# Indexer scores of a hybrid decoder step: from stacked 128-row products to pairs of 64-row tiles

## The chip, the core and the metric

One Trainium2 chip, of which one core runs the program. The metric is the device time of one execution in microseconds (us). TensorE is called PE in the profile (its weight loads are PEld), VectorE DVE, ScalarE ACT, GpSimd POOL, and SyncE SP.

## The reference, cut to what matters

One decoder layer runs over a prompt of 2048 positions and over 8 samples of 8 new positions each. The change is in the indexer, which scores every earlier key for each query and keeps the best 256:

```python
def indexer_scores(qi, wi, ki):          # 8 indexer heads x 64, one shared 64-wide key
    dots = jnp.einsum('bthd,bld->bthl', qi, ki)
    return jnp.einsum('bth,bthl->btl', wi, jax.nn.relu(dots))
```

For a block of 128 queries and L keys this is eight products with a contraction of 64, a relu each, and a weighted sum over the heads. Around it stand a combined input projection (2048 x 1024 by 1024 x 3656), attention over the chosen keys, a spatial gating group, an output projection and a gated embedding.

## The kernel before

All products are made to float32 accuracy out of float32r operands. A number is held as a rounded high part and the rest, its low part (`split`, lines 122 to 124: ACT makes the high part, DVE the low one), and the products of the parts are summed in PSUM.

The program has three phases. Phase A projects the 17 blocks (16 of the prompt, b = 0 to 15, and the samples) in three rounds (`ROUNDS`), chunk of columns by chunk of columns (`CH`, 14 of them). For each block and chunk, `proj` (lines 303, 304 and 306) runs 24 products of 128 rows into the PSUM tile `z`. In between, `pump` (in `phase_a`) feeds in steps of two chains: `idx`, which makes the scores of a block, and `topk`, which finds the 256th best score and writes a mask. Phase B does attention, phase C the output. The order in which the instructions finally stand on each engine is set by a list scheduler, which works with modelled times and moves an instruction to where it takes its operands and buffers to be ready. The five engines then run their lists in that order and wait for each other by semaphores.

In `idx` before, the key tile `ki_stack` holds the high parts of the 64 key components in rows 0 to 63 and the low parts in rows 64 to 127. The query of a head is loaded twice side by side, transposed and split (tiles `qih` and `qil`, lines 646, 123, 124). One product of 128 rows with `qih` (line 661) gives high x high plus high x low, a second with `qil` (line 662) gives low x high plus low x low. A head's scores for up to 1024 keys fill one buffer of the PSUM tile `dots`, of which there are two. ACT applies relu in place (line 664), and DVE adds the head to the score tile `big` (line 666) and so frees the buffer. The scores begin as minus the key's number times a tiny unit, made by POOL (line 652) from an int16 tile `iota` that is filled once (line 480).

Blocks 2 to 15 go through `idx`: 14 blocks with 3 to 16 times 128 keys, 133 x 128 = 17,024 keys in all. With 8 heads and 2 products this is 272,384 columns, in 608 products.

Of the kernel before, what the change touches and what calls it, by code (L numbers as in the profile page):

```python
# [9 lines left out]
F32 = mybir.dt.float32  # L10
F32R = mybir.dt.float32r
# [3 lines left out]
AF = mybir.ActivationFunctionType  # L15
OP = mybir.AluOpType
# [5 lines left out]
SEQ = 2048  # L22
NB = 16
SB = 16
PAST = 1024
WS = PAST + 64
# [4 lines left out]
UNIT = float(2.0 ** -110)  # L31
# [79 lines left out]
class Builder:  # L111
# [80 lines left out]
    def phase_a(self, eb):  # L192
        tc, nc, I, O = self.tc, self.nc, self.I, self.O
        with ExitStack() as es:
# [7 lines left out]
            ac = right("a_const", 1)  # L202
# [3 lines left out]
            hp = pool("a_h", 6)  # L206
# [23 lines left out]
            ident = self.ident  # L230
# [79 lines left out]
            later = []  # L310
# [19 lines left out]
            def post(name, b, z):  # L330
                P = self.rows(b)
                rt = ropet[:, b]
                if name == "x1":
                    w = z[:, 64:72]
                    if b == SB:
                        nc.vector.tensor_scalar(self.absw[:P, b], w, (8 * 64) ** -0.5, None, op0=OP.mult)
                    else:
                        nc.scalar.activation(self.absw[:P, b], w, AF.Abs, scale=(8 * 64) ** -0.5)
                        nc.scalar.activation(self.sgn[:P, b], w, AF.Sign)
                    kin2 = wk.tile([128, 2, 64], F32, name="kin")[:P]  # L340
                    nc.scalar.activation(kin2, z[:, None, 0:64].to_broadcast([P, 2, 64]), AF.Copy)
                    self.rope(nc.vector, kin2, rt, 2, wk, P)
                    kin = kin2[:, 0]
                    dst = O["idx_k_sample"].rearrange("o a t d -> (o a t) d") if b == SB else O["idx_k_prompt"][0, 0, b * 128:(b + 1) * 128]
                    nc.sync.dma_start(dst, kin)

                    def ki_t():
                        ps = self.tp.tile([128, 4, 128], F32, name="tp")
                        nc.tensor.transpose(ps[:, 0, :P], kin2.rearrange("p a d -> p (a d)"), ident[:P, :P])
# [4 lines left out]
                    later.append(ki_t)  # L354
# [74 lines left out]
            blocks_due, dots, tops = [], [], []  # L429
# [36 lines left out]
            for b in ROUNDS[0][1:]:  # L466
# [12 lines left out]
            iota = ac.tile([128, SEQ], mybir.dt.int16, name="iota")  # L479
            nc.gpsimd.iota(iota, pattern=[[1, SEQ]], base=0, channel_multiplier=0)  # L480
            self.iota = iota
# [81 lines left out]
            order = list(range(NB)) + [SB]  # L563
# [61 lines left out]
    def load_qi(self, b):  # L625
# [7 lines left out]
            out.append(qd)  # L633
        return out

    def idx(self, b):
        nc, wk, wk2 = self.nc, self.wk, self.wk2
        W = 128 * (b + 1)
        qds = self.load_qi(b)
        yield None  # L640
        qh, ql = [], []
        for j in range(2):
            qd = qds[j].rearrange("p h a d -> p h (a d)")
            ps = self.tp.tile([128, 4, 128], F32, name="tp")
# [5 lines left out]
            yield 2  # L650
        acc = self.big.tile([128, SEQ], F32, name="big")[:, :W]
        nc.gpsimd.tensor_scalar(acc, self.iota[:, :W], -UNIT, 1.0, op0=OP.mult, op1=OP.mult)
        kf = self.ki.rearrange("p a b -> p (a b)")
        for c0 in range(0, W, 1024):
            cn = min(1024, W - c0)
            for h in range(8):
                ps = self.dp.tile([128, 1024], F32, name="dots")
                for s0 in range(0, cn, 512):
                    sn = min(512, cn - s0)
                    rhs = kf[:, c0 + s0:c0 + s0 + sn]  # L660
                    nc.tensor.matmul(ps[:, s0:s0 + sn], lhsT=qh[h // 4][:, h % 4], rhs=rhs, start=True, stop=False)  # L661
                    nc.tensor.matmul(ps[:, s0:s0 + sn], lhsT=ql[h // 4][:, h % 4], rhs=rhs, start=False, stop=True)  # L662
                r = ps[:, :cn]
                nc.scalar.activation(r, r, AF.Relu)  # L664
                a = acc[:, c0:c0 + cn]
                nc.vector.scalar_tensor_tensor(a, r, self.sgn[:, b, h:h + 1], a, op0=OP.mult, op1=OP.add)  # L666
# [11 lines left out]
    def sample_idx(self):  # L678
        nc, wk2, I = self.nc, self.wk2, self.I
        V = nc.vector  # L680
        qi = wk2.tile([128, 4, 128], F32R, name="qih", bufs=3).bitcast(F32)
# [16 lines left out]
        pick = wk2.tile([128, 4, 128], F32R, name="qih", bufs=3)  # L698
# [7 lines left out]
        ps = self.tp.tile([128, 4, 128], F32, name="tp")  # L706
# [3 lines left out]
        ps = self.tp.tile([128, 4, 128], F32, name="tp")  # L710
# [5 lines left out]
        V.tensor_copy(knT, ps[:, 0, :64])  # L716
        yield 2
        acc = self.big.tile([128, SEQ], F32, name="big")
        pgs = {}

        def fetch(i):
# [8 lines left out]
        scs, behind = {}, []  # L730

        def second(c, p, n, kT):
            ds = self.tp.tile([128, 4, 128], F32, name="tp").rearrange("p a b -> p (a b)")[:, :n]
            nc.tensor.matmul(ds, lhsT=qi[:, p], rhs=kT[:, :n], start=True, stop=True)
            r = wk2.tile([128, 4, 128], F32R, name="qil", bufs=3).bitcast(F32).rearrange("p a b -> p (a b)")[:, :n]
            nc.scalar.activation(r, ds, AF.Relu)
            behind.append(lambda: third(c, p, n, r))

        def third(c, p, n, r):
            if p == 0:  # L740
                scs[c] = self.dp.tile([128, 1024], F32, name="dots")
            nc.tensor.matmul(scs[c][:64, :n], lhsT=G[:, p], rhs=r, start=(p == 0), stop=(p == 3))
            if p == 3:
                V.scalar_tensor_tensor(acc[:64, c * 512:c * 512 + n], self.iota[:64, c * 512:c * 512 + n], -UNIT,
                                       scs.pop(c)[:64, :n], op0=OP.mult, op1=OP.add)

        for c in range(3):
            n = 512 if c < 2 else 64
            for p in range(4):
                old = list(behind)  # L750
                behind.clear()
                for f in old:
                    f()
                if c < 2:
                    fetch(c * 4 + p + 1)
                    pg = pgs.pop(c * 4 + p)
                    ps = self.tp.tile([128, 4, 128], F32, name="tp")
                    for k in range(4):
                        nc.tensor.transpose(ps[:, k], pg[:, k].rearrange("p a d -> p (a d)"), self.ident)
                    kT = wk2.tile([128, 4, 128], F32R, name="qih", bufs=3).bitcast(F32).rearrange("p a b -> p (a b)")  # L760
# [788 lines left out]
```

## Time and profile before

| | us |
|---|---|
| Three timed runs | 1964.53, 1956.28, 1952.77 |
| Median of the three | 1956.28 |
| Span of the profiled execution, first to last instruction | 1952.4 |
| PE busy in it | 1865.8 (96%) |
| DVE, ACT, POOL busy | 1317.3, 995.7, 830.4 |
| Mean granted clock of TensorE, as a share of full speed | 0.985 |

No time of its own is given for the profiled execution beside its span; the median of the timed runs is 3.9 us above that span. Busy times of PE come from modelled ends: two products that follow each other overlap in the records, so what a product costs is read from the distance between two starts.

### The profile page before, as it was taken

How to read it: one execution, taken by the hardware profiler on the slowest of the kernel's cores; microseconds unless marked ns; L12 is line 12 of the kernel's file. 1: busy time of each engine (PE TensorE's matmuls, PEld its weight loads, DVE VectorE, ACT ScalarE, POOL GpSimd, SP SyncE). 2: the span in 40 equal slices, each digit the busy share in tenths (PEclk: the TensorE clock that was granted, in tenths of full speed). 3: DMA queues.
4: the chain of work that ended last, by engine and by line, in shares of the span. 5: the costliest groups of instructions: out<-in, count | busy, mean ns of one | idle time of the engine just before them, and what ended most of it. 6: DMA issues, size and time to landing. Idle time of an engine off the chain costs nothing. (4 is left out here: it accounts for less than half of the span.)

```text
span 1952.4 us, 35414 instructions
## 1 busy us (share of the span) xinstructions
PE 1865.8 (96%) x12370; PEld 1655.2 (85%) x12370; DVE 1317.3 (67%) x3682; ACT 995.7 (51%) x1907; POOL 830.4 (43%) x1323
## 2 busy tenths in 40 slices
PE   6989999899999899998999899999999999999998
PEld 5989989897998898997999778887788877888887
DVE  5496566488889758889752688888878865333321
ACT  3234325245555535665664788777867753122211
POOL 5482565554335679547513452213211155222311
PEclk9999999899999999998999999999999999999999
DMA  6423324423333432433455442222222064222311
GB/s 197 112 68 91 113 86 140 125 57 101 85 102 103 144 100 76 126 96 100 135 187 173 142 125 81 81 72 85 64 70 60 27 212 148 90 99 74 116 37 44
DMA packets 193687, 202.26 MB, mean 104 GB/s; under 512 B 85528, under 2 KB 160864, under 8 KB 193376
## 3 DMA queue, kind: packets, MB, share of 16 engines
q1 hardware_dynamic: 187872, 181.08, 30.9%
q0 software_dynamic: 5632, 18.88, 3.1%
q8 instruction: 98, 1.61, 0.4%
q14 instruction: 85, 0.70, 0.1%
HBM read 142.47 MB, written 57.42 MB: 102 GB/s over the span
## 5 line engine op out<-in xcount | busy, mean ns | idle before, releaser
L303 PE MATMUL z<-whi,hhi 128*128 128x256 f32 (+1 forms) x1792 | 461.3, 291 | 14.2 <-ACT qn L376 4.2
L304 PE MATMUL z<-wlo,hhi 128*128 128x256 f32 (+1 forms) x1792 | 455.0, 287 | 2.4 <-POOL wlo L276 2.4
L303 PEld LDWEIGHTS z<-whi,hhi 128*128 128x128 f32 x1792 | 342.7, 191 | 26.7 <-ACT qn L376 6.7
L304 PEld LDWEIGHTS z<-wlo,hhi 128*128 128x128 f32 x1792 | 342.7, 191 | 6.5 <-POOL wlo L276 2.7
L306 PE MATMUL z<-whi,hlo 128*128 128x256 f32 (+1 forms) x1792 | 269.6, 287 | 0.0
L275 POOL TENSOR_SCALAR whi<-raw 128x256 fp32r<-128x256 f32 (+1 forms) x332 | 151.2, 466 | 265.0 <-PE z L306 115.7
L306 PEld LDWEIGHTS z<-whi,hlo 128*128 128x128 f32 x1792 | 240.1, 189 | 4.8
L666 DVE SCALAR_TENSOR_TENSOR big<-dots,sgn,big 128x1024 f32<-128x1024 f32 (+7 forms) x176 | 178.7, 1016 | 43.3 <-ACT dots L664 42.6
L664 ACT ACTIVATE dots<-dots 128x1024 f32<-128x1024 f32 (+7 forms) x176 | 140.5, 801 | 118.4 <-PE dots L662 115.2
L124 DVE TENSOR_TENSOR b_pt<-b_tp,b_pt 128x512 fp32r<-128x512 f32 (+1 forms) x288 | 183.4, 656 | 14.1 <-ACT b_pt L123 12.0
L802 ACT ACTIVATE bfw<-big,tk 128x384 bf16<-128x384 f32 (+14 forms) x105 | 136.6, 1301 | 93.5 <-DVE tk L822 58.7
L123 ACT ACTIVATE b_pt<-b_tp 128x512 fp32r<-128x512 f32 (+1 forms) x288 | 156.1, 579 | 54.2 <-PE b_tp L1111 51.3
L1128 PE MATMUL b_o<-b_pt,Vst 128*128 128x512 f32 x544 | 182.9, 422 | 0.6 <-DVE b_pt L124 0.5
L1085 ACT ACTIVATE b_sm<-b_sm,b_st 128x128 f32<-128x128 f32 (+15 forms) x128 | 155.2, 1214 | 34.7 <-DVE b_st L1078 33.5
L1111 PE MATMUL b_tp<-mats,b_sm 128*128 128x128 f32 x1088 | 171.7, 274 | 0.3 <-ACT b_sm L1085 0.2
L1111 PEld LDWEIGHTS b_tp<-mats,b_sm 128*128 128x128 f32 x1088 | 132.2, 141 | 30.0 <-ACT b_sm L1085 2.0
L276 POOL TENSOR_TENSOR wlo<-raw,whi 128x256 fp32r<-128x256 f32 (+1 forms) x182 | 144.5, 803 | 6.2
L1076 PE MATMUL b_s<-Kst,b_qh 128*128 128x512 f32 (+3 forms) x320 | 139.8, 439 | 6.7 <-DVE b_st L1078 4.8
L1078 DVE CUSTOM_DVE_ANT_0 b_sm<-b_s,b_mask,b_st 128x512 f32<-128x512 f32 (+3 forms) x192 | 124.0, 646 | 23.9 <-PE b_s L1077 19.9
L661 PE MATMUL dots<-ki_stack,qih 128*128 128x512 f32 (+3 forms) x304 | 113.6, 376 | 10.7 <-DVE big L666 10.7
L1077 PE MATMUL b_s<-Kst,b_ql 128*128 128x512 f32 (+3 forms) x320 | 117.9, 371 | 0.1
L662 PE MATMUL dots<-ki_stack,qil 128*128 128x512 f32 (+3 forms) x304 | 111.9, 378 | 0.0
(344 smaller groups left out, 4095.4 us busy)
## 6 DMA issues: line engine op xcount, KB each, us to landing
raw<-w_in SPq DMA_DIRECT2D x336, 128.0 KB
x<-x_prompt SPq DMA_DIRECT2D x16, 512.0 KB
b_qr<-s_q SPq DMA_DIRECT2D x32, 256.0 KB
s_r<-hlo SPq DMA_DIRECT2D x32, 256.0 KB
c_r<-s_r SPq DMA_DIRECT2D x16, 512.0 KB
c_x<-x_prompt SPq DMA_DIRECT2D x16, 512.0 KB
y_prompt<-c_rn SPq DMA_DIRECT2D x15, 512.0 KB
qid<-s_qi SPq DMA_DIRECT2D x56, 128.0 KB
```

Source lines behind the costliest of these rows:

```text
L123: nc.scalar.activation(hi, src, AF.Copy)
L124: nc.vector.tensor_tensor(lo, src, hi.bitcast(F32), OP.subtract)
L275: nc.gpsimd.tensor_scalar(wh[:, k, :n], raw[:, :n], 1.0, 1.0, op0=OP.mult, op1=OP.mult)
L276: (nc.vector if k < WLO_DVE[r] else nc.gpsimd).tensor_tensor(wl[:, k, :n], raw[:, :n], wh[:, k, :n].bitcast(F32), OP.subtract)
L303: nc.tensor.matmul(z, lhsT=hh[:, k], rhs=wh[:, k, :n], start=(k == 0), stop=False)
L304: nc.tensor.matmul(z, lhsT=hh[:, k], rhs=wl[:, k, :n], start=False, stop=False)
L306: nc.tensor.matmul(z, lhsT=hl[:, k], rhs=wh[:, k, :n], start=False, stop=(k == 7))
L664: nc.scalar.activation(r, r, AF.Relu)
L666: nc.vector.scalar_tensor_tensor(a, r, self.sgn[:, b, h:h + 1], a, op0=OP.mult, op1=OP.add)
L1085: nc.scalar.activation(part, part, AF.Exp, bias=stt[:, h, c:c + 1], scale=-1.0, accum_out=stt[:, h, 4 + e:5 + e])
L1111: nc.tensor.transpose(ps[:, k, r], sm2[r][:, (k0 + k) * 128:(k0 + k) * 128 + 128], ident)
L1128: nc.tensor.matmul(o.rearrange("p a b -> p (a b)"), lhsT=Vst[:, kb, g].rearrange("p a d -> p (a d)"), rhs=pt[:, k].rearrange("p a b -> p ( ...
```

## The change

Two key tiles take the place of one. `ki_hi` holds the high parts twice, in rows 0 to 63 and again in rows 64 to 127; `ki_lo` holds the low parts twice. A query block is loaded once, and a transpose of 128 columns now brings two heads, one in rows 0 to 63 and one in rows 64 to 127. For each pair of heads there are three products per head (high x high, high x low, low x high; low x low is gone), each of 64 rows. The even head uses the upper half of the array, the odd head the lower half. The pair takes both `dots` buffers, and the program writes the products of the two heads in turn. The key numbers are now made by an iota for each block (`order`), and `qih` and `qil` have two buffers instead of three. The sample block's indexer only changes buffers.

```diff
-            self.ki = ac.tile([128, 17, 128], F32R, name="ki_stack")
+            self.kih = ac.tile([128, NB, 128], F32R, name="ki_hi")
+            self.kil = ac.tile([128, NB, 128], F32R, name="ki_lo")
...
-                        kst = self.ki[:, b, :P]
-                        nc.scalar.activation(kst, ps[:, 0, :P], AF.Copy)
-                        nc.vector.tensor_tensor(kst[64:128], ps[64:128, 0, :P], kst[64:128].bitcast(F32), OP.subtract)
+                        self.split(self.kih[:, b], self.kil[:, b], ps[:, 0])
...
+    def order(self, acc, P):
+        nc = self.nc
+        nc.gpsimd.iota(acc[:P], pattern=[[1, acc.shape[1]]], base=0, channel_multiplier=0,
+                       allow_small_or_imprecise_dtypes=True)
+        nc.gpsimd.tensor_scalar(acc[:P], acc[:P], -UNIT, 1.0, op0=OP.mult, op1=OP.mult)
...
-        qds = self.load_qi(b)
+        qd = wk2.tile([128, 4, 128], F32, name="qid", bufs=2)
+        nc.sync.dma_start(qd, self.s_qi[b].rearrange("p (h d) -> p h d", h=4))
...
-            for h in range(4):
-                nc.tensor.transpose(ps[:, h], qd[:, h], self.ident)
-            qh.append(wk2.tile([128, 4, 128], F32R, name="qih", bufs=3))
-            ql.append(wk2.tile([128, 4, 128], F32R, name="qil", bufs=3))
-            self.split(qh[j], ql[j], ps)
+        for j in range(4):
+            nc.tensor.transpose(ps[:, j], qd[:, j], self.ident)
+        qh = wk2.tile([128, 4, 128], F32R, name="qih", bufs=2)
+        ql = wk2.tile([128, 4, 128], F32R, name="qil", bufs=2)
+        self.split(qh, ql, ps)
...
-        nc.gpsimd.tensor_scalar(acc, self.iota[:, :W], -UNIT, 1.0, op0=OP.mult, op1=OP.mult)
+        self.order(acc, 128)
...
-            for h in range(8):
-                ps = self.dp.tile([128, 1024], F32, name="dots")
+            for j in range(4):
+                pss = [self.dp.tile([128, 1024], F32, name="dots") for _ in range(2)]
                 for s0 in range(0, cn, 512):
                     sn = min(512, cn - s0)
-                    rhs = kf[:, c0 + s0:c0 + s0 + sn]
-                    nc.tensor.matmul(ps[:, s0:s0 + sn], lhsT=qh[h // 4][:, h % 4], rhs=rhs, start=True, stop=False)
-                    nc.tensor.matmul(ps[:, s0:s0 + sn], lhsT=ql[h // 4][:, h % 4], rhs=rhs, start=False, stop=True)
-                r = ps[:, :cn]
+                    for n, (lhs, rhs) in enumerate(((qh, kh), (qh, kl), (ql, kh))):
+                        for e in range(2):
+                            hp = slice(e * 64, e * 64 + 64)
+                            nc.tensor.matmul(pss[e][:, s0:s0 + sn], lhsT=lhs[hp, j], rhs=rhs[hp, c0 + s0:c0 + s0 + sn],
+                                             start=(n == 0), stop=(n == 2))
...
-                yield cn / 128
+                yield cn / 64
```

The scheduler decides where the products of a pair stand. On PE before, in block 2 of the prompt (384 keys), one head's two products (`dots_1147`) stand between projection products (`z`):

```order
L306 MATMUL z_1121<-whi_792,hlo_293 128x256 x8
L661 MATMUL dots_1147<-ki_stack_217,qih_1101 128x384
L662 MATMUL dots_1147<-ki_stack_217,qil_1102 128x384
L303 MATMUL z_1157<-whi_792,hhi_315 128x256
L304 MATMUL z_1157<-wlo_793,hhi_315 128x256
```

On PE now, at the same place, `dots_1133` is the even head of a pair (upper half of the array) and `dots_1134` the odd one (lower half). Lines are one further on in the changed file, so that L304, L305 and L307 are the projection:

```order
L305 MATMUL z_1183<-wlo_792,hhi_339 128x256
L664 MATMUL dots_1133<-ki_hi_217,qih_1088 128x384
L664 MATMUL dots_1133<-ki_lo_218,qih_1088 128x384
L664 MATMUL dots_1133<-ki_hi_217,qil_1089 128x384
L304 MATMUL z_1183<-whi_791,hhi_339 128x256
L305 MATMUL z_1183<-wlo_792,hhi_339 128x256
L307 MATMUL z_1183<-whi_791,hlo_340 128x256
L664 MATMUL dots_1134<-ki_hi_217,qih_1088 128x384
L664 MATMUL dots_1134<-ki_lo_218,qih_1088 128x384
L664 MATMUL dots_1134<-ki_hi_217,qil_1089 128x384
L307 MATMUL z_1183<-whi_791,hlo_340 128x256 x7
```

The two heads of the pair, which the program writes in turn, were moved apart: each head's three products stand in a row, with 128-row products between the heads.

In a few places the pair stays together. On PE now, in block 3, where both `dots` buffers are taken as free (`dots_1593` even, `dots_1594` odd):

```order
L298 MATMUL z_1564<-wlo_1020,hhi_385 128x256
L664 MATMUL dots_1593<-ki_hi_217,qih_1364 128x512
L664 MATMUL dots_1594<-ki_hi_217,qih_1364 128x512
L664 MATMUL dots_1593<-ki_lo_218,qih_1364 128x512
L664 MATMUL dots_1594<-ki_lo_218,qih_1364 128x512
L664 MATMUL dots_1593<-ki_hi_217,qil_1365 128x512
L664 MATMUL dots_1594<-ki_hi_217,qil_1365 128x512
L304 MATMUL z_1639<-whi_1292,hhi_268 128x256
```

Here even and odd alternate, as written. In the whole list the 912 score products stand in 171 unbroken runs (before: 608 products in 178 runs). 156 of the runs, with 810 products, hold one head alone. In the other 15, 35 pairs of equal width stand even beside odd, 15,616 columns in each head.

## Rows read from the trace of the kernel before

**Rows 1.** Stretches: length, busy (count) of PE, PEld, DVE, ACT, POOL, clock, DMA.

```profile
75.00:970.00 895.00, 852.09 (x6308) 802.39 (x6307) 685.09 (x2137) 444.60 (x827) 506.77 (x852) 0.98 0.36 102
970.00:1093.00 123.00, 113.64 (x944) 110.70 (x942) 48.98 (x164) 65.71 (x114) 26.27 (x45) 1.00 0.51 164
```

**Rows 2.** Waits of PE, 75 to 970 us: total us, times, longest.

```profile
PE dots L661 <- DVE big L666: 10.7, 4, 6.8
PE tp L254 <- DVE hlo L124: 6.7, 2, 5.3
```

**Rows 3.** Page, part 5, the score steps: busy us, mean ns, idle before.

```profile
L666 DVE SCALAR_TENSOR_TENSOR big<-dots,sgn,big 128x1024 f32<-128x1024 f32 (+7 forms) x176 | 178.7, 1016 | 43.3 <-ACT dots L664 42.6
L664 ACT ACTIVATE dots<-dots 128x1024 f32<-128x1024 f32 (+7 forms) x176 | 140.5, 801 | 118.4 <-PE dots L662 115.2
```

**Rows 4.** Timeline of PE, one head's four score products: start us, us.

```profile
959.22 0.40 PE L661 MATMUL dots<-ki_stack,qih 128*128 128x512 f32 x1
...
960.15 0.28 PE L303 MATMUL z<-whi,hhi 128*128 128x256 f32 x1
```

**Rows 5.** Timeline of PE, products in column tiles (128*32), one tile and four.

```profile
1116.23 0.62 PE L1286 MATMUL b_s<-s_kT,s_QS 128*32 128x256 f32 x2
1116.78 0.44 PE L1111 MATMUL b_tp<-mats,b_sm 128*128 128x128 f32 x2
...
1154.18 0.64 PE L1286 MATMUL b_s<-s_kT,s_QS 128*32 128x256 f32 x8
1154.75 0.44 PE L1277 MATMUL b_tp<-mats,s_kpg 128*128 128x128 f32 x2
```

**Rows 6.** Timeline of PE, 64-row transposes (64*128) between 128-row products.

```profile
1773.48 0.39 PE L1432 MATMUL c_mm<-c_h_w_ple_gate,c_mh 128*128 128x512 f32 x1
1773.80 0.46 PE L1416 MATMUL c_tp<-mats,c_rn 64*128 64x64 f32 x4
1774.10 0.28 PE L1416 MATMUL c_tp<-mats,c_p 64*128 64x64 f32 x2
1774.31 0.50 PE L1433 MATMUL c_mm<-c_l_w_ple_gate,c_mh 128*128 128x512 f32 x1
1774.65 0.40 PE L1432 MATMUL c_mm<-c_h_w_ple_gate,c_mh 128*128 128x512 f32 x1
1774.88 0.40 PE L1433 MATMUL c_mm<-c_l_w_ple_gate,c_mh 128*128 128x512 f32 x1
```

**Rows 7.** Timeline of PE, four transposes of index queries, then projection.

```profile
71.51 0.60 PE L646 MATMUL tp<-mats,qid 128*128 128x128 f32 x4
71.86 0.36 PE L303 MATMUL z<-whi,hhi 128*128 128x256 f32 x1
72.06 0.28 PE L304 MATMUL z<-wlo,hhi 128*128 128x256 f32 x1
```

**Rows 8.** Timeline of PEld, weight loads of the stretch of Rows 4.

```profile
959.22 0.19 PEld L662 LDWEIGHTS dots<-ki_stack,qil 128*128 128x128 f32 x1
959.46 0.19 PEld L661 LDWEIGHTS dots<-ki_stack,qih 128*128 128x128 f32 x1
```

**Rows 9.** Tiles qih, qil: the split of index queries, ns min/median/max.

```profile
L123 ACT ACTIVATE qih<-tp x28: 575/597/613, 72.1 to 887.6; 128x512 fp32r<-128x512 f32 x28
L124 DVE TENSOR_TENSOR qil<-tp,qih x28: 666/681/693, 73.3 to 889.6; 128x512 fp32r<-128x512 f32 x28
```

**Rows 10.** Lines 480 and 652, key numbers on POOL: ns min/median/max.

```profile
L480 POOL IOTA iota<- x1: 1837/1837/1837, 0.8 to 0.8; 128x2048 int16 x1
...
L652 POOL TENSOR_SCALAR big<-iota x14: 512/1534/2032, 60.6 to 913.0; 128x384 f32<-128x384 int16 x1, 128x512 f32<-128x512 int16 x1, 128x640 f32<-128x640 int16 x1, 128x768 f32<-128x768 int16 x1
```

**Rows 11.** Timeline of PE, 128-row and 64-row products of 32 columns.

```profile
1235.36 0.97 PE L1331 MATMUL b_tp<-s_pt,s_vpg 128*128 128x32 f32 x8
1236.27 0.40 PE L1331 MATMUL b_tp<-s_pt,s_vn 64*128 64x32 f32 x2
1236.60 0.50 PE L1076 MATMUL b_s<-Kst,b_qh 128*128 128x512 f32 x1
```

More of the change, by code (lines that the diff above doesn't have):

```diff
@@ L348, in ki_t @@
                         ps = self.tp.tile([128, 4, 128], F32, name="tp")
-                        nc.tensor.transpose(ps[:, 0, :P], kin2.rearrange("p a d -> p (a d)"), ident[:P, :P])
-                        kst = self.ki[:, b, :P]
-                        nc.scalar.activation(kst, ps[:, 0, :P], AF.Copy)
-                        nc.vector.tensor_tensor(kst[64:128], ps[64:128, 0, :P], kst[64:128].bitcast(F32), OP.subtract)
-                    later.append(ki_t)
+                        nc.tensor.transpose(ps[:, 0], kin2.rearrange("p a d -> p (a d)"), ident)
+                        self.split(self.kih[:, b], self.kil[:, b], ps[:, 0])
+                    if b != SB:
+                        later.append(ki_t)
                 if name in ("x1", "x2"):
@@ L478, in phase_a @@
             nc.vector.tensor_scalar(qkg[:, 0], qkg[:, 0], -0.125, None, op0=OP.mult)
-            iota = ac.tile([128, SEQ], mybir.dt.int16, name="iota")
-            nc.gpsimd.iota(iota, pattern=[[1, SEQ]], base=0, channel_multiplier=0)
-            self.iota = iota
             io8 = tk.tile([128, 8], F32, name="io8")
@@ L640, in idx @@
         yield None
[L641 to L644, printed above, removed]
-            for h in range(4):
-                nc.tensor.transpose(ps[:, h], qd[:, h], self.ident)
-            qh.append(wk2.tile([128, 4, 128], F32R, name="qih", bufs=3))
-            ql.append(wk2.tile([128, 4, 128], F32R, name="qil", bufs=3))
-            self.split(qh[j], ql[j], ps)
-            yield 2
+        ps = self.tp.tile([128, 4, 128], F32, name="tp")
@@ L651, in idx @@
+        for j in range(4):
[3 more added lines that the diff above has]
+        self.split(qh, ql, ps)
+        yield 2
         acc = self.big.tile([128, SEQ], F32, name="big")[:, :W]
-        nc.gpsimd.tensor_scalar(acc, self.iota[:, :W], -UNIT, 1.0, op0=OP.mult, op1=OP.mult)
-        kf = self.ki.rearrange("p a b -> p (a b)")
+        self.order(acc, 128)
@@ L654, in idx @@
+        kh, kl = (t.rearrange("p a b -> p (a b)") for t in (self.kih, self.kil))
         for c0 in range(0, W, 1024):
             cn = min(1024, W - c0)
-            for h in range(8):
-                ps = self.dp.tile([128, 1024], F32, name="dots")
+            for j in range(4):
+                pss = [self.dp.tile([128, 1024], F32, name="dots") for _ in range(2)]
                 for s0 in range(0, cn, 512):
                     sn = min(512, cn - s0)
-                    rhs = kf[:, c0 + s0:c0 + s0 + sn]
-                    nc.tensor.matmul(ps[:, s0:s0 + sn], lhsT=qh[h // 4][:, h % 4], rhs=rhs, start=True, stop=False)
-                    nc.tensor.matmul(ps[:, s0:s0 + sn], lhsT=ql[h // 4][:, h % 4], rhs=rhs, start=False, stop=True)
-                r = ps[:, :cn]
-                nc.scalar.activation(r, r, AF.Relu)
-                a = acc[:, c0:c0 + cn]
-                nc.vector.scalar_tensor_tensor(a, r, self.sgn[:, b, h:h + 1], a, op0=OP.mult, op1=OP.add)
-                yield cn / 128
+                    for n, (lhs, rhs) in enumerate(((qh, kh), (qh, kl), (ql, kh))):
[3 more added lines that the diff above has]
+                                             start=(n == 0), stop=(n == 2))
+                for e in range(2):
+                    h = 2 * j + e
+                    r = pss[e][:, :cn]
+                    nc.scalar.activation(r, r, AF.Relu)
+                    a = acc[:, c0:c0 + cn]
+                    nc.vector.scalar_tensor_tensor(a, r, self.sgn[:, b, h:h + 1], a, op0=OP.mult, op1=OP.add)
+                yield cn / 64
@@ L680, in sample_idx @@
         V = nc.vector
-        qi = wk2.tile([128, 4, 128], F32R, name="qih", bufs=3).bitcast(F32)
+        qi = wk2.tile([128, 4, 128], F32R, name="qih", bufs=2).bitcast(F32)
         nc.gpsimd.memset(qi, 0.0)
@@ L697, in sample_idx @@
         gt = wk2.tile([128, 4, 2, 64], F32, name="qid", bufs=2).rearrange("p h a d -> p (h a d)")[:64]
-        pick = wk2.tile([128, 4, 128], F32R, name="qih", bufs=3)
+        pick = wk2.tile([128, 4, 128], F32R, name="qil", bufs=2)
         pick = pick.bitcast(F32).rearrange("p a b -> p (a b)")[:64, 0:64].rearrange("p (a b) -> p a b", a=8)
@@ L718, in sample_idx @@
         acc = self.big.tile([128, SEQ], F32, name="big")
+        self.order(acc[:, :WS], 64)
         pgs = {}
@@ L734, in second @@
             nc.tensor.matmul(ds, lhsT=qi[:, p], rhs=kT[:, :n], start=True, stop=True)
-            r = wk2.tile([128, 4, 128], F32R, name="qil", bufs=3).bitcast(F32).rearrange("p a b -> p (a b)")[:, :n]
+            r = wk2.tile([128, 4, 128], F32R, name="qil", bufs=2).bitcast(F32).rearrange("p a b -> p (a b)")[:, :n]
             nc.scalar.activation(r, ds, AF.Relu)
@@ L743, in third @@
             if p == 3:
-                V.scalar_tensor_tensor(acc[:64, c * 512:c * 512 + n], self.iota[:64, c * 512:c * 512 + n], -UNIT,
-                                       scs.pop(c)[:64, :n], op0=OP.mult, op1=OP.add)
+                a = acc[:64, c * 512:c * 512 + n]
+                V.tensor_tensor(a, scs.pop(c)[:64, :n], a, OP.add)
         for c in range(3):
@@ L759, in sample_idx @@
                         nc.tensor.transpose(ps[:, k], pg[:, k].rearrange("p a d -> p (a d)"), self.ident)
-                    kT = wk2.tile([128, 4, 128], F32R, name="qih", bufs=3).bitcast(F32).rearrange("p a b -> p (a b)")
+                    kT = wk2.tile([128, 4, 128], F32R, name="qih", bufs=2).bitcast(F32).rearrange("p a b -> p (a b)")
                     nc.scalar.activation(kT.rearrange("p (x k) -> p x k", k=4), ps.rearrange("p k x -> p x k"), AF.Copy)
```

2 lines of the change are left out of this document (1 added, 1 removed).

## The prediction

> **What bounds the kernel now.** I read the page's engine totals first, then the table of stretches, then the waits of PE, and last the timeline of PE around the scores. Indexer scores are made from 75 to 970 us. In these 895 us PE is busy for 852.1, DVE for 685.1, POOL for 506.8 and ACT for 444.6 [rows 1]. So PE bounds the stretch, and it idles for 42.9 us. Its waits are short and of many kinds: the longest, for a `dots` buffer that DVE has not yet freed, comes to 10.7 us in all, the next to 6.7 [rows 2]. DVE and ACT wait for each other and for PE: relu was held up by a PE product for 115.2 us in all [rows 3]. Hence time added to PE from 75 to 970 us lengthens the run almost one for one, and work taken off DVE or ACT there gives nothing. Later stretches keep their instructions.
>
> **The change part by part.**
>
> *Score products.* Four products of 512 columns start at 959.22, and the next instruction at 960.15: 0.93 us, 0.232 each [rows 4]. At that rate the 272,384 columns of before cost 272,384 / 2048 x 0.93 = 123.7 us. The change has three products for each head instead of two, 408,576 columns. A product of 64 rows streams as many columns as one of 128. So the products gain only if the two heads of a pair run at the same time, and that needs them to stand side by side in PE's list. The order shows them so for 35 pairs alone; 810 of 912 products stand in runs of one head, with 128-row products between these runs. One after the other the products cost 408,576 / 2048 x 0.93 = 185.5 us. If the 35 pairs do overlap, 15,616 / 2048 x 0.93 = 7.1 us come off. Rows of before do not show row tiles at the same time. Column tiles they do: a step with one tile takes 1116.78 - 1116.23 = 0.55 us, a step with four tiles 0.57 [rows 5]. I take the overlap: 178.4 us, **+54.7**; without it +61.8.
>
> *Switches between 128-row and 64-row products.* A run of score products is now of another shape than what stands on either side. The trace has that step in phase C, where 64-row transposes stand between 128-row products [rows 6]. Going in: the last 512-column product starts at 1773.48 and the transposes at 1773.80, 0.32 us against the usual 0.23, so 0.09 are lost. Coming out: a transpose of 128 columns takes 0.108 us [rows 7], so one of 64 columns should take 0.054; the last two took 1774.31 - 1774.10 = 0.21, so 0.10 are lost again. Then the first 512-column product takes 1774.65 - 1774.31 = 0.34 us, 0.11 more than the next, which has 0.23: its weights were not loaded ahead. The first product inside should pay for its weights in the same way. The low end of that is the first four transposes, 0.30 us where 4 x 0.054 = 0.22 were due: 0.08. The high end is 0.11, and I take it, since the first product after the switch has the type and the number of weight columns of a score product. A run then costs 0.09 + 0.11 + 0.10 + 0.11 = 0.41 us, 0.38 at the low end. With 171 runs that is **+70.1 us** (+65.0). Before, the runs had the shape of their neighbours and paid nothing: 959.22 to 960.15 has no gap [rows 4].
>
> *Weights within a run.* In the full array the weights of the next product are loaded while the last one streams: the load for line 662 starts at 959.22 together with the product of line 661 [rows 8, 4], and products still follow at 0.23. I take it that this holds within a row tile; the four 64-row transposes, 0.30 us in all [rows 6], speak for it. The Trainium skill, "TensorE: Matmul & The Clock Gate", section "The mechanism", states that a weight load overlaps products in flight only where the row group differs. That would make every product in a run of one head wait for its weights. The two sets of rows above, with one row group throughout, don't agree with it; the sum by it is the third rival below.
>
> *Transposes.* A block now has 4 instead of 8: 56 fewer. Four of them and one 256-column product (0.12) take 72.06 - 71.51 = 0.55 us [rows 7], so one is 0.108: **-6.0 us** on PE.
>
> *Off PE.* Each of the 14 blocks loses one of two splits: 14 x 0.60 us on ACT and 14 x 0.68 on DVE [rows 9], 8.4 and 9.5 us on engines that wait for PE, so nothing. Splitting a key block needs the same two instructions as before; nothing. SP issues one load for a block instead of four; nothing, it holds up no one here. POOL gets an iota for each of 15 blocks. One over 2048 keys took 1.84 us [rows 10]; by width (18,112 in all) they come to 18,112 / 2048 x 1.84 = 16.3 us. The multiplication after it was there before. POOL has 388 us to spare in the stretch [rows 1], and weight splits queued behind an iota are late by at most 2 us. Zero; +16 if that cover were gone. `qih` with two buffers instead of three is enough, since a block takes one instead of two.
>
> *What PE's idle time takes up.* Of the 42.9 us of idle, the 10.7 for `dots` should go, as DVE gets more time between two runs. Of the other 32 I let a third go, since ACT and DVE will be further ahead of a slower PE: **-20**. The bounds are 0 and -42.9.
>
> *Sum.* 54.7 + 70.1 - 6.0 - 20 = +99 us on the span of 1952.4, so 2051. The median of the timed runs is 3.9 above that span: **2055 us**, 5% slower. With low switches and all idle time used it is 54.7 + 65.0 - 6.0 - 42.9 = +71, or 2027. With no overlap, no idle time used and POOL's iota bare it is 61.8 + 70.1 - 6.0 + 16 = +142, or 2098.
>
> **The rivals.**
>
> *Cheaper switches and full use of idle time.* Between a score product and a projection product, both float32r, the going out might cost only one of its two parts, and 42.9 us of idle might vanish. That is 54.7 + 171 x 0.30 - 6.0 - 42.9 = +57: 2013. For it: PE's waits are spread over many small causes [rows 2]. Against it: lines 1432 and 1433, before and after the transposes, are float32r too and lose 0.09 and 0.11 [rows 6].
>
> *The pairs run at the same time after all.* Then all products cost 185.5 / 2 = 92.8 us, and a pair is one run: 88 of them, 88 x 0.41 = 36.1. With the transposes that is 92.8 + 36.1 - 6.0 - 123.7 = -0.8, or 1955: no change, since the switches eat what the overlap gives. Against it is the order: heads are apart.
>
> *Each product in a run waits for its weights.* Of 912 products 741 are not the first of their run; at 0.11 they add 81.5 us: 2136. The rule of the Trainium skill quoted above would do this. Against it are the 64-row transposes and the weight loads [rows 6, 8].
>
> *Not slower: a 64-row product costs by its rows.* If half the rows took half the time, 0.116 us for 512 columns, the products would cost 92.8 us, one head after the other. With switches, transposes and idle time as above: 92.8 + 70.1 - 6.0 - 20 - 123.7 = +13, or 1969, within 1%. It decides below 0.124 us for 512 columns, where the sum is +20. Against it: eight 128-row products of 32 columns took 0.91 us up to the switch, at most 0.11 each, and two 64-row ones 0.33 with 0.10 of it for the switch, 0.12 each [rows 11].
>
> **How the numbers follow.** A measurement of this kernel tells about 1% from no change; 1% of the median is 19.6 us. My forecast, with its own spread of 2027 to 2098, has a chance of 0.63; cheaper switches 0.19; weights exposed (or new waits of that size) 0.09; pairs at once 0.03; cost by rows 0.03; and 0.03 for a gain of over 1% that I can't name. The predicted time is 2055. The range is 2000 to 2098: it holds the forecast and the cheaper switches. Faster: 0.03. Same: 0.06, the two cases at 1955 and 1969. Slower: 0.91.
>
> **What the changed profile would show.** PE's score products (line 664 there) start 0.23 us apart within a run of one head, and almost together in the 35 pairs. Before the first of a run and after the last, PE loses 0.2 us each. The end of the scores moves from 970 to about 1069 us, and phases B and C keep their lengths. PE's wait for `dots` falls below 10 us. I am wrong if score products in a run stand much closer than 0.23, if the first projection product after a run takes its usual 0.12, or if the stretch grows by less than PE's added work because idle time shrinks by far more than 20 us.

## The result, and the profile after

The changed kernel takes 2049.54 us (median of 4 runs, 2044.23 to 2055.50) against 1955.55 for the kernel before on the same chip: 1.0472 times as long, with a 95% interval of 1.0439 to 1.0504. That is 94 us slower. The forecast was 2055. The profiled execution, the longest of the four, has a span of 2053.7 us, 101.3 more than before.

The first product of phase B (tile `b_s`) started at 1084.46 us before and starts at 1181.45 in this execution, 97.0 later. Not all of that is the change. By 75 us, 296 projection products had started before and 260 here, so a stretch from 75 us does not hold equal work. Part of that shows in the stretch from 25 to 50 us, of before and then of the changed kernel (columns as in [rows 1]): 122 products and a granted clock of 0.93, then 107 and 0.77.

```profile
25.00:50.00 25.00, 19.95 (x122) 18.57 (x123) 16.30 (x40) 8.47 (x27) 15.59 (x35) 0.93 0.54 161
```

```profile
25.00:50.00 25.00, 19.22 (x107) 17.43 (x106) 15.01 (x34) 9.26 (x28) 14.71 (x31) 0.77 0.50 145
```

Projection product 297 starts at 75.40 us before and at 79.67 here. In a kernel below that differs from the changed one in POOL's work alone it starts at 75.16, so these 4.3 us need not come with the change. From that product to phase B both kernels have the same 6104 projection products. Before, and then now:

```profile
75.40:1084.46 1009.06, 960.26 (x7214) 908.82 (x7214) 730.48 (x2278) 504.52 (x923) 531.25 (x894) 0.98 0.37 109
```

```profile
79.67:1181.45 1101.78, 1070.32 (x7469) 950.38 (x7468) 724.48 (x2265) 501.43 (x912) 551.99 (x909) 0.99 0.33 98
```

PE is busy for 1070.32 - 960.26 = 110.1 us more. It idles for 1101.78 - 1070.32 = 31.5 us where it idled for 48.8, so 17.3 less. The difference, 92.7 us, is what the stretch has grown by. DVE and ACT have no more work than before, and POOL's 21 us more lie beside PE. PE bounds the stretch in both kernels, and its work grew.

The waits of PE from 75 to 1070 us, the longest and the only one of score products:

```profile
PE z L297 <- ACT qn L376: 4.7, 1, 4.7
...
PE dots L664 <- DVE qil L124: 1.0, 1, 1.0
```

The wait for a `dots` buffer, 10.7 us in [rows 2], is gone; score products wait for 1.0 us in all, for the split of a query block. The relu (line 669 now) waits for PE more than in [rows 3], 179.4 us against 115.2; it is a follower.

Now PE's timeline around one run of score products, one head and 256 keys. Columns: start, length, line, operation.

```profile
600.07 1.11 PE L307 MATMUL z<-whi,hlo 128*128 128x256 f32 x8
601.11 0.38 PE L664 MATMUL dots<-ki_hi,qih 64*128 64x256 f32 x1
601.34 0.28 PE L664 MATMUL dots<-ki_lo,qih 64*128 64x256 f32 x1
601.46 0.28 PE L664 MATMUL dots<-ki_hi,qil 64*128 64x256 f32 x1
601.66 0.38 PE L304 MATMUL z<-whi,hhi 128*128 128x256 f32 x1
601.89 0.28 PE L305 MATMUL z<-wlo,hhi 128*128 128x256 f32 x1
602.00 0.28 PE L304 MATMUL z<-whi,hhi 128*128 128x256 f32 x1
```

Read the starts. A product of 256 columns is due 0.12 us after the one before it, as 601.34 to 601.46 and 601.89 to 602.00. The first of the run takes 601.34 - 601.11 = 0.23, the last 601.66 - 601.46 = 0.20, and the first projection product behind it 601.89 - 601.66 = 0.23. Eight products from 600.07 fill 0.94 us, and the run starts 1.04 after them: 0.10 more. So the shape costs at four places. The weight loads (PEld) say why the first product of each shape is slow:

```profile
601.11 0.18 PEld L664 LDWEIGHTS dots<-ki_hi,qih 64*128 64x128 f32 x1
...
601.34 0.18 PEld L664 LDWEIGHTS dots<-ki_hi,qil 64*128 64x128 f32 x1
601.66 0.19 PEld L304 LDWEIGHTS z<-whi,hhi 128*128 128x128 f32 x1
```

The load at 601.34 starts together with the product before its own; those at 601.11 and 601.66 start no earlier than their own product. Nothing is loaded ahead across a change of shape.

A place where the two heads of a pair stand side by side (x2 is one product for each head):

```profile
115.02 0.49 PE L664 MATMUL dots<-ki_hi,qih 64*128 64x512 f32 x2
115.35 0.39 PE L664 MATMUL dots<-ki_lo,qih 64*128 64x512 f32 x2
115.58 0.40 PE L664 MATMUL dots<-ki_hi,qil 64*128 64x512 f32 x2
115.91 0.39 PE L304 MATMUL z<-whi,hhi 128*128 128x256 f32 x1
```

Two products take the 0.23 us of one. There are 36 such places in the trace, 1 to 22 ns between the two starts, at most 6 in 32 of them.

### The profile page after: what moved, and what is told of

Its sections match the earlier page's. It is cut to its first block, busy times and chain, and to the rows that moved or that the text cites. A ratio compares the mean times of both kernels' runs of the same rounds, so it can differ in the third digit from the quotient of the medians.

```text
span 2053.7 us, 35809 instructions
## 1 busy us (share of the span) xinstructions
PE 1980.4 (96%) x12617; PEld 1701.8 (83%) x12617; DVE 1309.6 (64%) x3667; ACT 992.3 (48%) x1892; POOL 850.1 (41%) x1338
## 5 line engine op out<-in xcount | busy, mean ns | idle before, releaser
L304 PE MATMUL z<-whi,hhi 128*128 128x256 f32 (+1 forms) x1792 | 468.2, 295 | 11.3 <-ACT qn L376 3.2
L305 PE MATMUL z<-wlo,hhi 128*128 128x256 f32 (+1 forms) x1792 | 462.4, 291 | 2.0 <-POOL wlo L277 2.0
L304 PEld LDWEIGHTS z<-whi,hhi 128*128 128x128 f32 x1792 | 343.5, 192 | 37.5 <-issue 19.5
L305 PEld LDWEIGHTS z<-wlo,hhi 128*128 128x128 f32 x1792 | 343.5, 192 | 17.8 <-issue 12.7
L307 PE MATMUL z<-whi,hlo 128*128 128x256 f32 (+1 forms) x1792 | 271.8, 289 | 0.0
L307 PEld LDWEIGHTS z<-whi,hlo 128*128 128x128 f32 x1792 | 237.5, 190 | 13.5 <-issue 10.3
L669 ACT ACTIVATE dots<-dots 128x1024 f32<-128x1024 f32 (+7 forms) x176 | 139.9, 799 | 184.5 <-PE dots L664 179.4
L664 PE MATMUL dots<-ki_hi,qih 64*128 64x512 f32 (+3 forms) x304 | 123.4, 424 | 0.0
L1439 PE MATMUL c_mm<-c_l_w_ple_gate,c_mh 128*128 128x512 f32 x272 | 106.9, 393 | 2.6 <-DVE c_l_w_ple_gate L1392 2.6
```

The source lines that it names most:

```text
L304: nc.tensor.matmul(z, lhsT=hh[:, k], rhs=wh[:, k, :n], start=(k == 0), stop=False)
L305: nc.tensor.matmul(z, lhsT=hh[:, k], rhs=wl[:, k, :n], start=False, stop=False)
L307: nc.tensor.matmul(z, lhsT=hl[:, k], rhs=wh[:, k, :n], start=False, stop=(k == 7))
L1439: nc.tensor.matmul(z, lhsT=hi[:, k], rhs=wts[k][1][:, ns], start=False, stop=(b == SB and k == nk - 1))
```

## The experiments

**Theories.** Mine: the loss is PE's, and has two parts. Three products for each head instead of two, nearly all one after the other, and 171 runs that pay for two changes of shape each. Rival A: a change of shape costs nothing, and the added products are all of the loss. Rival B: PE has room, and the loss comes from waits or from POOL. One table first; times are medians in us, the kernel before is that of the same chip, and PE's busy and idle time are from the start of projection product 297 to the first product of phase B. That stretch holds the same projection products in every kernel. The time that the granted clock spends at its lower level in it differs, from 20 to 41 us in all kernels but the last, which has 181; so I take a difference of PE's busy time to be good to some 5 us, an estimate.

| kernel | time | before | difference | ratio, 95% interval | PE busy | PE idle |
|---|---|---|---|---|---|---|
| before | | | | | 960.3 | 48.8 |
| the change | 2049.5 | 1955.6 | +94.0 | 1.0472 (1.0439 to 1.0504) | 1070.3 | 31.5 |
| third product | 2003.4 | 1952.9 | +50.5 | 1.0250 (1.0227 to 1.0272) | 1021.1 | 40.8 |
| 64-row product between, 128 columns | 2026.6 | 1952.9 | +73.7 | 1.0366 (1.0338 to 1.0394) | 1039.6 | 39.4 |
| 128-row product between, 128 columns | 1980.2 | 1954.5 | +25.7 | 1.0111 (1.0082 to 1.0141) | 982.5 | 52.6 |
| 128-row product between, 256 columns | 1972.9 | 1958.2 | +14.7 | 1.0086 (1.0057 to 1.0115) | 980.9 | 45.5 |
| 64-row product between, 256 columns | 2026.6 | 1958.2 | +68.4 | 1.0359 (1.0328 to 1.0390) | 1046.1 | 36.0 |
| iota three times | 2043.9 | 1952.9 | +91.1 | 1.0464 (1.0442 to 1.0485) | 1068.6 | 29.8 |
| pairs, 512 keys | 1986.4 | 1952.9 | +33.5 | 1.0171 (1.0150 to 1.0192) | 982.7 | 55.3 |
| pairs, 1024 keys | 2087.9 | 1954.5 | +133.4 | 1.0691 (1.0657 to 1.0725) | 975.2 | 167.7 |

**The third product alone.** The kernel before, with zeros kept in key block 16, which no score reads:

```diff
+            self.zero = self.ki[:, SB]
+            nc.vector.tensor_scalar(self.zero, self.ident, 0.0, None, op0=OP.mult)
...
                     nc.tensor.matmul(ps[:, s0:s0 + sn], lhsT=qh[h // 4][:, h % 4], rhs=rhs, start=True, stop=False)
+                    nc.tensor.matmul(ps[:, s0:s0 + sn], lhsT=self.zero, rhs=rhs, start=False, stop=False)
                     nc.tensor.matmul(ps[:, s0:s0 + sn], lhsT=ql[h // 4][:, h % 4], rhs=rhs, start=False, stop=True)
```

> The kernel before, with a third product of 128 rows for each head and chunk, whose stationary operand is all zeros: 912 score products as in the changed kernel, but none of 64 rows, so no switches (one transpose of an unused key block falls away). What it adds is worth nothing to the output and is there for its time alone. My theory: 304 more products at 0.232 us for 512 columns add 61.8 us to PE, PE's idle time takes up 15 to 20 of it, so about 1955 + 45 = 2000 us. Rival A, that switches cost nothing and the third products are the whole loss of 94 us: about 2050. Rival B, that PE has room and the loss came from waits or from POOL: 1955 to 1965.

2003.4 us, as my theory has it; about half of the loss. PE's timeline shows the zero product at the common pace of 0.23 us:

```profile
799.62 0.39 PE L664 MATMUL dots<-ki_stack,qih 128*128 128x512 f32 x1
799.85 0.40 PE L665 MATMUL dots<-ki_stack 128*128 128x512 f32 x1
800.08 0.40 PE L666 MATMUL dots<-ki_stack,qil 128*128 128x512 f32 x1
```

PE is busy for 60.8 us more (61.8 due), and its idle time gives back 8.0, half of what I had put down. Rivals A (2050) and B (1955 to 1965) are both out. What is left of the 94 us needs another cause.

**Switches alone.** The same zeros, as one short product of 64 rows in each head chunk:

```diff
                     nc.tensor.matmul(ps[:, s0:s0 + sn], lhsT=qh[h // 4][:, h % 4], rhs=rhs, start=True, stop=False)
+                    if s0 == 0:
+                        nc.tensor.matmul(ps[:, :128], lhsT=self.zero[:64], rhs=rhs[:64, :128], start=False, stop=False)
```

> The kernel before, with one product of 64 rows and 128 columns, all zeros, put between the two products of each of the 176 head chunks: two switches for each head chunk and next to no added columns. Its product adds zeros and is there for its time alone. My theory: 176 x (0.40 us for going in and out, with the weights that are not loaded ahead, + 0.06 for the product itself) = 81 us on PE, of which idle time takes up 15 to 20: about 1955 + 63 = 2018 us. Rival A, switches free: 176 x 0.06 = 10.6 us at most, 1955 to 1966. Rival: a switch costs only one of its two sides: 176 x 0.26 = 46, less idle time: about 1983.

2026.6 us: 176 tiny products cost 73.7 us, 8.6 more than expected, since idle time gave back 9.4 and not 15 to 20. PE's timeline:

```profile
802.90 0.39 PE L664 MATMUL dots<-ki_stack,qih 128*128 128x512 f32 x1
803.22 0.32 PE L666 MATMUL dots<-ki_stack 64*128 64x128 f32 x1
803.47 0.50 PE L667 MATMUL dots<-ki_stack,qil 128*128 128x512 f32 x1
803.80 0.39 PE L664 MATMUL dots<-ki_stack,qih 128*128 128x512 f32 x1
```

Two products that take 0.46 us take 0.90 with 128 columns of 64 rows between them. Is it the rows, or would any product in between cost that? The control has all 128 rows in that product:

```diff
-                        nc.tensor.matmul(ps[:, :128], lhsT=self.zero[:64], rhs=rhs[:64, :128], start=False, stop=False)
+                        nc.tensor.matmul(ps[:, :128], lhsT=self.zero, rhs=rhs[:, :128], start=False, stop=False)
```

> The same as the run with a zero product of 64 rows between the two products of each head chunk, but that product now has 128 rows, so that the shape never changes; still 128 columns, its own weights, and zeros. My theory, that the price lies in the change of shape: 176 x 0.06 = 10.6 us on PE, of which idle time takes up some: 1953 to 1963 us. Rival, that any product put in between with weights of its own costs 0.4 us: about 2026, as with 64 rows.

1980.2 us: not the 2026 of the rival, but more than my 1953 to 1963. The timeline shows what I had left out:

```profile
801.97 0.39 PE L664 MATMUL dots<-ki_stack,qih 128*128 128x512 f32 x1
802.20 0.22 PE L666 MATMUL dots<-ki_stack 128*128 128x128 f32 x1
802.26 0.45 PE L667 MATMUL dots<-ki_stack,qil 128*128 128x512 f32 x1
802.55 0.22 PE L664 MATMUL dots<-ki_stack,qih 128*128 128x128 f32 x1
```

The zero product takes its 0.06 us, but the next one 802.55 - 802.26 = 0.29 instead of 0.23. With 0.577 us for the three where 0.464 was due without the zero product, a median of each, that makes about 20 of the 26 us; idle time grew by 3.8. If weights take 0.11 us to load and a product of 0.06 hides only that much of it, 0.05 stay bare. A longer product should then be free of it, except at a change of shape. Two more kernels have 256 columns there, with 128 rows and with 64:

```diff
-                        nc.tensor.matmul(ps[:, :128], lhsT=self.zero, rhs=rhs[:, :128], start=False, stop=False)
+                        nc.tensor.matmul(ps[:, :min(256, sn)], lhsT=self.zero, rhs=rhs[:, :min(256, sn)], start=False, stop=False)
```

```diff
-                        nc.tensor.matmul(ps[:, :128], lhsT=self.zero[:64], rhs=rhs[:64, :128], start=False, stop=False)
+                        nc.tensor.matmul(ps[:, :min(256, sn)], lhsT=self.zero[:64], rhs=rhs[:64, :min(256, sn)], start=False, stop=False)
```

> The control with a zero product of 128 rows once more, now with 256 columns instead of 128 (128 in the 8 chunks that have no more). The control with 128 columns took 26 us where I had expected 10; its trace shows a head's two products with the zero product between them at 0.58 us where 0.46 + 0.06 were due. My theory: a product of 0.06 us hides only half of the 0.11 us that the next product's weights take, and one of 256 columns (0.12 us) hides all of it: again 0.58 us for each head chunk, the same time within 5 us as with 128 columns, 1975 to 1985 us, though PE has 21,504 more columns (9.8 us). Rival, that an inserted product has a fixed price of 0.06 us beside its columns: 0.64 us for each, 1985 to 1995.

> The zero product of 64 rows between the two products of each head chunk, now with 256 columns instead of 128 (128 in the 8 chunks that have no more). My theory: at a change of shape no weights are loaded ahead, so a longer product hides nothing more, and its columns add in full: 168 x 0.058 = 9.8 us on PE, 2026.6 + 10 = about 2036 us; in the trace 0.49 us more for each head chunk than without it, 0.44 with 128 columns. Rival, that the longer product hides weights at a change of shape too: 2024 to 2030 us, as with 128 columns.

With 128 rows: 1972.9 us, 2 below my range and no slower than with half the columns, so the rival with a fixed price is out. The same place in the two timelines, 128 rows and then 64:

```profile
804.14 0.39 PE L664 MATMUL dots<-ki_stack,qih 128*128 128x512 f32 x1
804.37 0.28 PE L666 MATMUL dots<-ki_stack 128*128 128x256 f32 x1
804.49 0.40 PE L667 MATMUL dots<-ki_stack,qil 128*128 128x512 f32 x1
804.72 0.23 PE L664 MATMUL dots<-ki_stack,qih 128*128 128x128 f32 x1
```

```profile
804.33 0.39 PE L664 MATMUL dots<-ki_stack,qih 128*128 128x512 f32 x1
804.65 0.38 PE L666 MATMUL dots<-ki_stack 64*128 64x256 f32 x1
804.96 0.50 PE L667 MATMUL dots<-ki_stack,qil 128*128 128x512 f32 x1
805.30 0.39 PE L664 MATMUL dots<-ki_stack,qih 128*128 128x512 f32 x1
```

Over 120 such places in each trace the medians are 0.232, 0.118 and 0.232 us with 128 rows, 0.326, 0.311 and 0.339 with 64. The difference is the price of one going in and out: 0.09 before the 64-row product, 0.19 in it (0.10 for its weights, 0.09 for the way out), 0.11 in the product behind it, **0.39 us** together. PE's busy time gives nearly the same: (1046.1 - 980.9) / 176 = 0.37. For 64 rows the run's total is 2026.6, as with half the columns: inside the rival's 2024 to 2030, and 9 below my 2036. The timeline decides against the rival all the same: 0.311 us for the zero product, 0.254 with 128 columns, so the added columns are paid in full at each place. Of the 9.8 us due, PE's busy time shows 6.5, and idle time gave back 3.4 (36.0 against 39.4); the stretch is 3.1 us longer, and in the profiled execution it started 3.3 us sooner.

**POOL's added work.** The changed kernel, with its iota issued three times:

```diff
+        for _ in range(3):
-        nc.gpsimd.iota(acc[:P], pattern=[[1, acc.shape[1]]], base=0, channel_multiplier=0,
-                       allow_small_or_imprecise_dtypes=True)
+            nc.gpsimd.iota(acc[:P], pattern=[[1, acc.shape[1]]], base=0, channel_multiplier=0,
+                           allow_small_or_imprecise_dtypes=True)
```

> The changed kernel, with the iota of each block issued three times on POOL (two of them without effect on the output): 33 us more on POOL from 75 to 1070 us, nothing more on PE. My theory, that what the change adds to POOL is covered: no change from the changed kernel, 2044 to 2056 us. Rival, that POOL's work is on the path through the splitting of weights: +16 to +33, 2066 to 2082 us; the single iota would then be 8 to 16 us of the loss.

The groups of iotas, first of the changed kernel and then of this one. One of the 15 belongs to the sample block, whose indexer thus changes by more than its buffers.

```profile
L635 POOL IOTA big<- 128x384 f32 (+14 forms) x15 | 18.0, 1200 | 28.2 <-ACT dots L669 17.1 <-DVE v L844 10.6 <-issue 0.4
```

```profile
L636 POOL IOTA big<- 128x384 f32 (+14 forms) x45 | 52.0, 1157 | 34.6 <-DVE v L845 34.3
```

34 us more on POOL leave the time where it was: 1.0464 against 1.0472. What the change adds on POOL is covered.

**Pairs side by side.** The changed kernel, with both heads in one PSUM tile, 512 keys at a time. The scheduler then keeps the six products of a pair together.

```diff
-        for c0 in range(0, W, 1024):
-            cn = min(1024, W - c0)
+        for c0 in range(0, W, 512):
+            cn = min(512, W - c0)
...
-                pss = [self.dp.tile([128, 1024], F32, name="dots") for _ in range(2)]
...
+                ps = self.dp.tile([128, 2, 512], F32, name="dots")
+                for n, (lhs, rhs) in enumerate(((qh, kh), (qh, kl), (ql, kh))):
+                    for e in range(2):
+                        hp = slice(e * 64, e * 64 + 64)
+                        nc.tensor.matmul(ps[:, e, :cn], lhsT=lhs[hp, j], rhs=rhs[hp, c0:c0 + cn],
+                                         start=(n == 0), stop=(n == 2))
+                r = ps[:, :, :cn]
+                nc.scalar.activation(r, r, AF.Relu)
```

> The changed kernel, but with both heads of a pair in one PSUM tile of two banks, for 512 keys at a time, and one relu over both: the six products of a pair then stand side by side in 148 runs, and 759 neighbours of 912 alternate between the row tiles. My theory: the products run two at a time, 92.8 us, and 148 switches cost 148 x 0.40 = 59 us, so against the kernel before PE has 92.8 + 59 - 6 - 123.7 = +22 us, of which idle time takes up 10 or so: 1957 to 1977, most likely 1967 us. Rival, that row tiles side by side save nothing: 185.5 + 59 - 6 - 123.7 = +115, less 20 of idle time: about 2050, as the changed kernel.

1986.4 us, 63 less than the changed kernel, and far from the rival's 2050; but 33.5 slower than before, outside my 1957 to 1977. One run of a pair in PE's timeline:

```profile
765.48 0.28 PE L305 MATMUL z<-wlo,hhi 128*128 128x256 f32 x1
765.69 0.50 PE L662 MATMUL dots<-ki_hi,qih 64*128 64x512 f32 x2
766.02 0.39 PE L662 MATMUL dots<-ki_lo,qih 64*128 64x512 f32 x2
766.25 0.39 PE L662 MATMUL dots<-ki_hi,qil 64*128 64x512 f32 x2
766.58 0.38 PE L304 MATMUL z<-whi,hhi 128*128 128x256 f32 x1
766.80 0.28 PE L305 MATMUL z<-wlo,hhi 128*128 128x256 f32 x1
```

Six products take three times 0.23 us, and the four places of a change of shape are there again. PE's busy time is 22.4 us more than before, where I had +22. What I had wrong is the idle time: it did not fall by 10, it rose by 6.5. The longest waits of PE:

```profile
PE z L304 <- ACT qn L376: 12.1, 9, 2.3
PE dots L662 <- DVE big L669: 4.1, 7, 1.3
```

Waits in front of score products make 15.3 us in this trace, on DVE above all, 10.7 before; waits of projection products for a tile `qn` that ACT makes come to 12.1, 4.2 before. DVE has more additions here, 304 instead of 176, as each covers 512 keys at most; that this is why the waits grew was not tried.

**Pairs and half as many runs.** The changed kernel, with a pair in one PSUM tile for 1024 keys:

```diff
-            self.dp = pool("a_dots", 2, space=PSUM)
+            self.dp = pool("a_dots", 1, space=PSUM)
...
-                pss = [self.dp.tile([128, 1024], F32, name="dots") for _ in range(2)]
+                both = self.dp.tile([128, 2, 1024], F32, name="dots")
+                pss = [both[:, 0], both[:, 1]]
```

> The changed kernel, with both heads of a pair in one PSUM tile of four banks, 1024 keys at a time. That tile takes all of the pool's space, so there is one buffer instead of two. The products stand in 81 runs, 50 of them of 12 products, but the scheduler leaves the last 12 pairs to the end, where they stand in a row of 144 products and each pair waits for the one buffer. My theory: for PE, 92.8 + 81 x 0.40 - 6 - 123.7 = -5 us against the kernel before; at the end each of 12 pairs waits for a relu and two additions on DVE (1.01 + 1.28 + 1.28, about 4 us), +49 us. Together about 1953 - 5 + 49 = 1997 us, 1985 to 2010, and outside that last row of products the time up to it is that of the kernel before within 10 us. Rival, that the price isn't one for each run but one for each product of 64 rows (0.065 for each of 912, as 59 us over the 912 of the run with 512 keys would be): 92.8 + 59 - 6 - 123.7 + 49 = +71, about 2024.

2087.9 us: the slowest of all, and 90 more than I expected. In PE's work my theory holds: 975.2 us, 14.9 more than before, where a slower clock in the last row of products costs 16.7 (32.7 us for what takes 16 at 0.23). At full clock that is about -2, against my -5; the rival with a price for each product has +22. So 81 switches eat almost all that the pairs save. The loss is idle time, 167.7 us. The stretches before, in and behind the last row of products:

```profile
75.00:1022.00 947.00, 889.17 (x6916) 819.81 (x6915) 643.87 (x2029) 415.38 (x804) 528.61 (x878) 0.98 0.33 100
1022.00:1121.00 99.00, 34.13 (x156) 23.80 (x154) 48.48 (x115) 38.04 (x40) 2.66 (x2) 0.53 0.14 44
1121.00:1220.00 99.00, 53.88 (x418) 51.44 (x416) 40.21 (x125) 46.48 (x72) 18.50 (x33) 0.76 0.30 92
```

From 1022 to 1121 us each of 12 pairs waits for the one buffer, and the granted clock is 0.53:

```profile
1036.70 0.80 PE L665 MATMUL dots<-ki_hi,qih 64*128 64x512 f32 x2 [4.39 <-DVE big L672]
1037.27 0.66 PE L665 MATMUL dots<-ki_lo,qih 64*128 64x512 f32 x2
1037.69 0.66 PE L665 MATMUL dots<-ki_hi,qil 64*128 64x512 f32 x2
```

Two things were not in my estimate. The clock: products of 512 columns now start 0.43 us apart. And what stands behind the scores: from 1121 us to phase B PE idles for 99.00 - 53.88 = 45 us, of which one wait of phase B's first transposes for `Kst` on DVE has 32.9; which work holds DVE up there was not tried. Up to 1022 us the idle time was already 947.00 - 889.17 = 58.

## Why the prediction held, point by point

**PE bounds the stretch.** Right. Over equal work the stretch grew by 92.7 us, and the sum had +99. From phase B's first product to PE's last product it is 865 us, 861 before.

**Score products, +54.7.** The trace has 81.4 us more from the starts of score products to the next starts, idle time left out. Of that 171 x 0.198 = 33.9 belong to the switches (medians: 0.107 in a run's first product, 0.091 in its last), so the products cost **+47.5**. The third product alone cost +60.8 on PE, where 61.8 were due. The forecast was 7 us too high because its 123.7 us for the products before was too low: the trace of before has 131.4, and 131.4 + 47.5 = 178.9 meets the 178.4 forecast for the products now. The 123.7 rests on four products at 0.232 [rows 4], and some run slower: products of 512 columns make 6.0 of the 7.7 us. Two stretches of the kernel before, and its timeline in the second:

```profile
446.00:450.00 4.00, 1.72 (x7) 1.02 (x7) 3.93 (x24) 2.22 (x6) 2.69 (x5) 0.76 0.35 91
451.00:453.30 2.30, 2.30 (x6) 1.73 (x6) 2.27 (x17) 1.57 (x2) 1.62 (x2) 0.50 0.79 211
```

```profile
451.17 0.63 PE L661 MATMUL dots<-ki_stack,qih 128*128 128x512 f32 x1
451.60 1.05 PE L662 MATMUL dots<-ki_stack,qil 128*128 128x512 f32 x2
```

These start 0.43 us apart, at a granted clock of 0.50, the lower of its two levels (1.2 GHz); it fell while PE was busy for 1.72 of 4 us. Products of 128 columns, many with 0.11 us instead of 0.06, for the weights that they don't hide, are the other part, 1.6 us.

**The 35 pairs.** Right: 36 places with two products at once, and six for the price of three when all pairs stand together.

**Switches, +70.1.** Right. Medians over the runs of the changed kernel are 0.092 + 0.107 + 0.091 + 0.106 = 0.396 us, 171 x 0.396 = **67.7**; forecast 0.09 + 0.11 + 0.10 + 0.11. The 64-row transposes of phase C [rows 6] gave the price to 4%. Two kernels that differ in nothing but the rows of one product confirm it at 0.39. The Trainium skill, "TensorEngine Tiling (Array Packing)", section "Key Properties", states that changing the tiling mode drains TensorE. The trace agrees: 0.09 us are lost ahead of each change. The larger half of the price, 0.11 us each time for weights that are not loaded ahead, the trace shows beside it. Around the runs, projection products gained 31.0 us over equal work where about 33.9 were due; why 2.9 less was not looked for, but the stretch of before spent 34.1 us at the lower level of the clock and this one 23.9.

**Weights within a run.** Right: 601.34 to 601.46 above, and a median of 0.232 for 512 columns in one row tile. By the rule of the Trainium skill that the prediction quoted, from "TensorE: Matmul & The Clock Gate", the time would have been near 2136; the measurement decides against it here.

**Transposes, -6.0.** PE's time on transposes (tile `tp`) fell by 2.6 us only: those of index queries by 4.6, while the others took 2.1 more, for a reason that was not looked for. A small miss.

**Off PE, nothing.** Shown for POOL, by 34 us more on it at no cost. DVE and ACT have 6.0 and 3.1 us less work in the stretch than before.

**Idle time, -20.** It was -17.3, and the wait for a `dots` buffer, 10.7 us before, is gone as forecast. But the size was a guess that happened to fit: in four experiments on the kernel before, with 21 to 86 us more on PE, idle time gave back 3.3 to 12.8 us; in two more kernels it rose by 3.8 and 6.5, and with one buffer by 119.

**End of the scores.** The last score product starts at 1046.4 us, not at 1069. Of the 23 us, 17 now stand behind the scores, where phase B follows after 135 us instead of 117: 96 more projection products (11.3 us) and 3.9 us more idle time, among others. That changes the order, not the sum. The rest is that the last one before started at 966.7, not 970, and that phase B moved by 97 us, not 99.

Together, with what the trace has for the projection products around the runs: 47.5 + 33.9 + 31.0 - 2.6 - 17.3 = +92.5, of 92.7 us. The forecast was 6 us higher: it had the score products 7 us and the switches 5 us too high (64.9 by this count), and took about 3 us too much off for the transposes and again for idle time.

## What to carry to other kernels

Price a change of tile shape by runs, not by products: here one run in another shape cost 0.39 us, and side by side a pair of heads took three times 0.23 us for 512 keys where it took four before, so a run has to hold two such pairs only to break even. Row tiles help only if the products of both tiles stand next to each other in PE's list, and two PSUM tiles let a scheduler pull them apart, while one tile kept them together. Buying longer runs with the second buffer left the kernel 133 us slower than before, more than the change itself.

## What the runs showed of the hardware that was not expected

In these runs a product hid its successor's weights only for as long as it streamed: behind 128 columns (0.06 us) the next product of 512 columns took 0.286 us, behind 256 columns 0.232, so that 256 columns put in between cost PE no more than 128 (0.583 and 0.577 us for the three products). Twice the columns were free here.

In the last row of products of the kernel with one buffer, PE was busy for 34 of 99 us, and the granted clock was 0.53, mostly the lower level of 1.2 GHz; it had been 0.98 in the stretch ahead, with PE busy for 889 of 947 us. Score products of 512 columns took 0.43 us there instead of 0.23.
